# Sample attention with the probabilities as stationary operand in four column groups, and another order of the first loads and of x's transposes, squares and spills

## The chip, the cores and the metric

The kernel runs on one core of a Trainium2 chip. The core has five engines with queues of their own: PE (TensorE, the matrix unit; PEld is its weight load), DVE (VectorE), ACT (ScalarE), POOL (GpSimd) and SP (SyncE, which here only issues DMAs). Time is device time in microseconds (us) of one execution; smaller is better.

## The reference

One inference step of one hybrid decoder layer for a prompt of 512 tokens and for 8 sample sequences of 4 tokens (32 tokens). Everything is float32.

```python
h = rmsnorm(x)                                   # D = 1024
x_r, q, k, v, g_lru, g_attn = split(h @ w_in)    # 1024, 1024, 256, 256, 1024, 1024 columns
A = rg_lru(causal_conv4(x_r))                    # gated recurrence
B = window_attention(q, k, v)                    # 8 query heads, 2 kv heads, window 128, sinks,
                                                 # relative-position bias from rel_bias (32 buckets)
m = (sigmoid(g_lru) * (A @ w_lru_o) + sigmoid(g_attn) * (B @ w_attn_o)) @ w_out
x = x + rmsnorm(m)
u = causal_conv3(rmsnorm(x) @ w_up)              # 2 x 4096 columns
x = x + rmsnorm((gelu(u_gate) * u_val) @ w_down)
```

For a sample sequence the attention runs over 128 cached keys and values and its own 4 new ones, `o = softmax([q·k_cache, q·k_new] + bias) · [v_cache, v_new]`. The outputs are both groups' rows and their new states.

## The kernel before, in words

**Operands.** Activations lie transposed: features on the 128 partitions, the 544 tokens (512 + 32) in the free dimension, cut into a half of 256 (a = 0) and one of 288 (a = 1). To keep float32 precision, each operand is split into a high and a low part (`hH`, `hL`, `wh_in`, `wl_in`), and each product is made of three: high·high, low·high, high·low. ACT makes the high part, DVE subtracts it and so makes the low one.

**Steps.** The work on PE is a row of steps. `step(key, X, a, done)` is one column block of 128 of a weight matrix times one half of the tokens: 24 matmuls into one PSUM bank of the pool PM (3 banks; tiles `pmin`, `pmao` and so on). After a step comes `tick()`: it splits the next weight pieces (`wsplit_hi` on ACT, L277; `wsplit_lo` on DVE, L282), advances the side work (generators that `start_at(t, ...)` enters at tick t; a `yield` waits for the next tick), evicts the step's result, and at its end runs what was put in the list `last`. Side work takes its banks from the pool PX (5 banks). The written order is the order of each of PE, ACT, DVE and POOL; SP's order is made by a scheduler from the order and the dependencies of its DMAs.

**The start.** The first steps all use the half a = 0, which needs tiles 0 and 1 of x only (`trans_a`, in `first_step`). Their weight pieces are w16, w18, w8, w9, w10, w11 in this order (the numbers are column blocks; tiles `raw_in_...` of 512 KB). Tiles 2, 3 (prompt) and 4 (the 32 sample rows) are loaded in two half tiles of 512 columns each (`xload(i, z)`, z the half) and make the other half of the tokens: `trans_b` transposes them on PE, three transposes into one bank `ps_tb` for each of 8 feature blocks k, `hsplit` makes `hH` and `hL` of each, and `keep_b` copies the bank to an SBUF tile `xk`, which a POOL DMA spills to DRAM (`xtd`), where x is read again for the residual. `row_scales` makes the squares of x's rows and the roots of their means.

**The bias table.** One small product on PE (`ps_ohp`, from `ohp` and `relx`, in `attn_tables`, behind the third step) gives the biases by distance; DVE copies it (`rvec`), a POOL DMA writes it to DRAM (`rscr`), a second one repeats it there 128 times for each head (`rrep`), and a third loads it as `btab` for the attention (`load_btab`), whose first use of it is a DVE operation into `s`.

**The sample attention.** `sample_attn(g)` runs for two groups g of four sequences each, in side work. The scores of the group (`pss`) are a matmul with the 32 columns of one sequence's q as weights, for each of four column groups of PE's array. The probabilities are transposed (`pst`) and copied to `spt`. Then the output, transposed, is made in one bank `pso`: the new values for all sequences at once, and for each sequence b and kv head the cached values as 128x128 weights (`cache_win_v`), with the 16 probability columns of that pair as the moving operand. ACT and DVE then split the bank head by head into `aH` and `aL`, the operands of the attention output product (`pmao`).

Of the kernel before, what the change touches and what calls it, by code (L numbers as in the profile page):

```python
# [117 lines left out]
def hawk_step(ctx, tc, I, O):  # L118
# [21 lines left out]
    def T(name, dt=F32):  # L140
        return tp.tile([P, FLAT + 4], dt, tag="t", name=name)
# [7 lines left out]
    def PX(name):  # L149
        return psx.tile([P, 512], F32, tag="aux", name=name)  # L150
# [4 lines left out]
    def f32(ap):  # L155
        return ap.bitcast(F32)

    def mm(out, l, r, start, stop):
        pe.matmul(out, l, r, start=start, stop=stop)  # L159

    def sub(out, a, b):
        dve.tensor_tensor(out=out, in0=a, in1=b, op=ALU.subtract)  # L162
# [216 lines left out]
    relx = cp.tile([NBK + 1, NH], F32, name="relx")  # L379
    ohp = T("ohp")[:NBK + 1, 0:3 * WIN]  # L380

    pool.memset(relx, 1.0)
    nc.sync.dma_start(out=relx[0:NBK, :], in_=I["rel_bias"])
    nc.sync.dma_start(out=ohp, in_=I["c_ohp"])

    def table_loads():
        pool.memset(lt, 0.0)
# [27 lines left out]
    ss = cp.tile([P, 4, 5], F32, name="ss")  # L415
    dve.memset(ss, 1.0)
    rsc = cp.tile([P, 4], F32, name="rsc")
    rep = cp.tile([P, NT], F32, name="rep")
    xtd = drp.tile([KD, P, NT], F32, name="xtd")

    jk, jv = T("jk"), T("jv")

    def xsquares(i):
        n = TOK[i][1]
        act.activation(jk[:n, 0:512], xt[i, 0][:n, 0:512], AF.Square, accum_out=ss[:n, 0, i:i + 1])
        xb = xt[i, 1][:n, 0:512]
        dve.scalar_tensor_tensor(out=jv[:n, 0:512], in0=xb, scalar=1.0, in1=xb, op0=ALU.mult, op1=ALU.mult,
                                 accum_out=ss[:n, 1, i:i + 1])
# [4 lines left out]
    def hsplit(k, a, ps):  # L433
        g = pv[:, G_PRE + k:G_PRE + k + 1]
        act.activation(h.get(k, a, 0), ps, AF.Copy, scale=g)
        stt(h.get(k, a, 1), ps, g, f32(h.get(k, a, 0)), ALU.mult, ALU.subtract)

    def xkeep(ks, lo, hi, src, copy):

        n = hi - lo  # L440
        t_ = S(f"xk{ks.start}_{lo}")[:, 0:n * (2 if lo == 0 else 1)]
        copy(t_, src)
        pool.dma_start(out=xtd[ks, :, lo:hi].rearrange("k p n -> p k n"), in_=t_.rearrange("p (k n) -> p k n", n=n))

    pta = {}

# [14 lines left out]
    ptb = {}  # L461

    def keep_b(k):
        xkeep(slice(k, k + 1), 256, NT, ptb.pop(k)[:, :288], act.copy if k % 4 else dve.tensor_copy)

    def trans_b():
        for k in range(KD):
            ps = ptb[k] = (PM if k == 5 else PX)(f"ps_tb{k}")
            for i in (2, 3, 4):
                pe.transpose(ps[:, (i - 2) * P:(i - 1) * P], xtile(i, k), ident)  # L470
# [10 lines left out]
    def row_scales():  # L481
        last.extend(lambda i=i: xsquares(i) for i in range(2))
        yield 3
        last.extend(lambda i=i: xsquares(i) for i in range(2, 5))
# [4 lines left out]
        dg = T("dg_x")  # L489
        for i in range(5):  # L490
            w = TOK[i][1]
            dve.tensor_scalar(dg[:, i * P:i * P + w], ident[:, :w], ss[:, 1, i:i + 1], None, ALU.mult)
        yield 2
        px = [PX(f"ps_rep{a}") for a in range(2)]
        for a in range(2):
            mm(px[a][:, 0:HN], ones, dg[:, a * HN:(a + 1) * HN], True, True)
        for a in range(2):
            act.copy(rep[:, a * HN:(a + 1) * HN], px[a][:, 0:HN])

# [289 lines left out]
    def sample_attn(g):  # L789
# [54 lines left out]
        for hd in range(NH):  # L844
            oh, ol = (A.t[hd][z][:, SEQ + 16 * g:SEQ + 16 * g + 16].rearrange("p (b t) -> p b t", b=4)
                      for z in range(2))
            act.activation(oh, ov[:, :, hd, :], AF.Copy)
            sub(ol, ov[:, :, hd, :], f32(oh))
# [143 lines left out]
    def first_step():  # L992
        key = order[0]
        ps = PM("pm_first")
        def parts(z):
            split_a(z, range(1))
            lows = [wsplit_hi(w) for w in wclaim(z + 1)]
            split_a(z, range(1, 4))
            for v in lows:
                wsplit_lo(*v, pool)  # L1000

        k03, k47 = range(4), range(4, 8)
        trans_a(0)
        parts(0)
        mmhalf(ps, key, h, 0, k03, (0, 1))
# [837 lines left out]
```

## Time and profile before

| | before |
|---|---|
| time, median of 3 runs | 1014.81 us (1013.72, 1014.81, 1015.28) |
| time of the profiled execution | 1013.11 us |
| its span (first to last instruction) | 1011.0 us |
| mean granted clock of PE | 0.992 |
| PE busy | 990.1 us, 7817 instructions |
| DVE, ACT, POOL busy | 734.8, 597.4, 164.7 us |
| the pso records (32 of 128x16) | mean 0.263 us each, from 185.8 to 203.0 us |

The profiled execution is one run, 1.70 us below the median of the three. The times in the trace count from the start of its span. In the rows below, L159 is the helper that records every matmul, so a place is told by its tile: `pmin` is the input projection, `ps_ohp` the bias product, `ps_tb` the transposes of tiles 2 to 4, `pss` and `pso` the sample attention. A matmul of float32 shows as two records of the same tile, and a row with xN is a run of N records alike. "[1.09 <-DMA ohp...]" is idle time of the engine ahead of the row and what ended it. In rows of stretches of time the columns are: start and end, length, PE busy with the number of matmuls begun, granted clock (1.00 is full), busy share of the DMA engines, GB/s.

### The profile page before, as it was taken

What the parts mean: (1) busy time and instruction counts of PE and PEld (TensorE: products, weight loads), DVE (VectorE), ACT (ScalarE), POOL (GpSimd) and SP (SyncE); (2) the same over time, 40 slices, a digit from 0 to 9 for tenths busy, and PEclk for the clock granted to TensorE, in tenths of its full rate; (3) what the DMA queues carried; (4) which work ended last, traced back from release to release, by engine and by line L of the source; (5) the groups of instructions that cost most, each with busy time, mean ns of one, the idle gap of its engine ahead of it and who ended that gap; (6) DMA issues with size and microseconds to landing.
All of it is one profiled execution on the core that took longest, in us unless ns stands there. A gap on an engine that the chain in (4) does not pass through costs nothing.

```text
span 1011.0 us, 20259 instructions
## 1 busy us (share of the span) xinstructions
PE 990.1 (98%) x7817; PEld 980.5 (97%) x7817; DVE 734.8 (73%) x1535; ACT 597.4 (59%) x1448; POOL 164.7 (16%) x284
## 2 busy tenths in 40 slices
PE   8999999999999999999999999999999999999996
PEld 7999999999999999999999999999999999999996
DVE  4666666676856755578877788888888888878855
ACT  5645655666668535545866656565655555655644
POOL 4242000120404442200001111111110101011003
PEclk9999999999999999999999999999999999999998
DMA  9842223232322535225045858586767777675612
GB/s 264 255 166 85 81 64 105 84 105 84 85 84 85 172 104 145 71 74 182 22 123 130 186 131 192 124 191 130 185 142 172 152 162 162 152 180 136 190 57 89
DMA packets 209204, 134.00 MB, mean 133 GB/s; under 512 B 6664, under 2 KB 195481, under 8 KB 209076
## 3 DMA queue, kind: packets, MB, share of 16 engines
q1 hardware_dynamic: 198516, 110.08, 38.5%
q0 software_dynamic: 10240, 20.08, 11.7%
q10 hardware_dynamic: 352, 2.56, 0.6%
q8 instruction: 61, 1.00, 0.4%
q14 instruction: 35, 0.29, 0.1%
HBM read 111.30 MB, written 11.37 MB: 121 GB/s over the span
## 4 chain that ended last, share of the span: by engine, by line
PE 83%; DVE 6%; ACT 4%; DMA 3%; issue 2%; SPq 1%; POOL 0%; POOLq 0%; DVEq 0%; ACTq 0%
PE pmin L159 19%; PE pmdn L159 18%; PE pux L1452 14%; PE puy L1452 7%; PE pmao L159 5%; PE pmlo L159 4%; PE pmout L159 4%; PE puz L1452 4%; PE pq L1452 2%; PE psc L159 1%; DVE uc L171 1%; DMA raw_up_s<-in_w_up_dram 1%; PE pvp L159 1%; PE pg L159 1%; SPq L254 1%
## 5 line engine op out<-in xcount | busy, mean ns | idle before, releaser
L159 PE MATMUL pmin<-hH,wh_in 128*128 128x256 f32 (+1 forms) x568 | 165.6, 293 | 0.3 <-ACT gl L1031 0.3
L159 PE MATMUL pmin<-hH,wl_in 128*128 128x256 f32 (+1 forms) x568 | 163.2, 289 | 0.3 <-DVE wl_in L282 0.3
L159 PE MATMUL pmin<-hL,wh_in 128*128 128x256 f32 (+1 forms) x568 | 162.9, 289 | 0.0
L159 PE MATMUL pmdn<-fH,wh_dn 128*128 128x256 f32 (+1 forms) x512 | 148.0, 289 | 0.0
L159 PE MATMUL pmdn<-fH,wl_dn 128*128 128x256 f32 (+1 forms) x512 | 147.3, 288 | 0.4 <-DVE wl_dn L162 0.4
L159 PE MATMUL pmdn<-fL,wh_dn 128*128 128x256 f32 (+1 forms) x512 | 147.5, 288 | 0.0
L171 DVE SCALAR_TENSOR_TENSOR uc<-u,fv,uc 128x560 f32<-128x560 f32 x128 | 101.8, 796 | 11.0 <-ACT uc L1483 10.8
L159 PEld LDWEIGHTS pmin<-hH,wh_in 128*128 128x128 f32 x568 | 107.7, 190 | 2.1 <-issue 0.6
L159 PEld LDWEIGHTS pmin<-hL,wh_in 128*128 128x128 f32 x568 | 107.6, 190 | 0.0
L159 PEld LDWEIGHTS pmin<-hH,wl_in 128*128 128x128 f32 x568 | 107.0, 189 | 0.5 <-DVE wl_in L282 0.5
L159 PEld LDWEIGHTS pmdn<-fH,wl_dn 128*128 128x128 f32 x512 | 96.3, 188 | 0.7 <-DVE wl_dn L162 0.7
L159 PEld LDWEIGHTS pmdn<-fH,wh_dn 128*128 128x128 f32 x512 | 96.4, 188 | 0.1
L159 PEld LDWEIGHTS pmdn<-fL,wh_dn 128*128 128x128 f32 x512 | 96.3, 188 | 0.1
L1578 ACT COPY u<-pux 128x272 f32<-128x272 f32 x52 | 20.1, 386 | 84.7 <-PE pux L1452 84.7
L168 DVE TENSOR_TENSOR ft<-ft,pmdn 128x256 f32<-128x256 f32 (+1 forms) x112 | 48.5, 433 | 28.0 <-PE pmdn L159 28.0
L162 DVE TENSOR_TENSOR u<-puy,u 128x240 f32<-128x240 f32 (+2 forms) x78 | 24.6, 343 | 50.4 <-PE puy L1452 31.9
L277 ACT ACTIVATE wh_in<-raw_in 128x512 fp32r<-128x512 f32 x72 | 43.9, 627 | 10.7 <-DMA raw_in<-in_w_in_dram 6.3
L1483 ACT ACTIVATE uc<-u,fv 128x560 f32<-128x560 f32 x64 | 48.4, 755 | 1.8 <-DVE u L1459 1.8
L282 DVE TENSOR_TENSOR wl_in<-raw_in,wh_in 128x512 fp32r<-128x512 f32 x70 | 47.4, 694 | 0.0
L162 DVE TENSOR_TENSOR wl_dn<-raw_dn,wh_dn 128x512 fp32r<-128x512 f32 x64 | 43.7, 683 | 1.3 <-ACT wh_dn L1389 1.3
L1389 ACT ACTIVATE wh_dn<-raw_dn 128x512 fp32r<-128x512 f32 x64 | 39.7, 623 | 3.3 <-DMA raw_dn<-in_w_down_dram 3.3
L159 PE MATMUL pmlo<-lH,wh_lo 128*128 128x272 f32 x128 | 37.1, 290 | 1.3 <-ACT gl L1031 1.3
(747 smaller groups left out, 3323.4 us busy)
## 6 DMA issues: line engine op xcount, KB each, us to landing
raw_in<-in_w_in_dram SPq DMA_DIRECT2D x35, 512.0 KB
raw_dn<-in_w_down_dram SPq DMA_DIRECT2D x56, 256.0 KB
raw_up_s<-in_w_up_dram SPq DMA_DIRECT2D x26, 512.0 KB
raw_up_s<-raw_up_s POOLq DMA_DIRECT2D x26, 256.0 KB, 5.4
raw_ao<-in_w_attn_o_dram SPq DMA_DIRECT2D x8, 512.0 KB
raw_lo<-in_w_lru_o_dram SPq DMA_DIRECT2D x8, 512.0 KB
raw_out<-in_w_out_dram SPq DMA_DIRECT2D x8, 512.0 KB
x<-xtd SPq DMA_DIRECT2D x8, 272.0 KB
```

The source lines that it names most:

```text
L159: pe.matmul(out, l, r, start=start, stop=stop)
L162: dve.tensor_tensor(out=out, in0=a, in1=b, op=ALU.subtract)
L168: dve.tensor_tensor(out=out, in0=a, in1=b, op=ALU.add)
L171: dve.scalar_tensor_tensor(out=out, in0=a, scalar=s_, in1=b, op0=op0, op1=op1)
L254: nc.sync.dma_start(out=raw, in_=wsrc(key))
L277: act.activation(hl[0], raw, AF.Copy)
L282: (eng or dve).tensor_tensor(out=hl[1], in0=raw, in1=f32(hl[0]), op=ALU.subtract)
L1389: act.activation(hl[0], src, AF.Copy)
L1452: pe.matmul(ps[:, :HN], w, x, start=start and k == 0 and i == 0, stop=stop and k == 3 and i == 2, skip_group_check=True)
L1483: act.activation(yt[j][:, 0:FLATU], u[:, 0:FLATU], AF.Copy, scale=fv[:, j:j + 1])
L1578: act.copy(e[nm_], z)
```

## The change

**The first loads (SP).** `ohp` and `relx` are loaded ahead of and behind w8's piece, and tiles 2 to 4 of x by halves: the z = 0 halves ahead of w9's piece, the z = 1 halves ahead of w10's. In SP's queue, before; `raw_in_18` is w18's piece, and so on:

```order
L254 DMA raw_in_18_112<-in_w_in_dram 128x8x128
L254 DMA raw_in_8_114<-in_w_in_dram 128x8x128
L254 DMA raw_in_9_116<-in_w_in_dram 128x8x128
L254 DMA raw_in_10_118<-in_w_in_dram 128x8x128
L365 DMA x2_0_120<-in_x_prompt_dram 128x512
L365 DMA x2_1_122<-in_x_prompt_dram 128x512
L365 DMA x3_0_124<-in_x_prompt_dram 128x512
L365 DMA x3_1_126<-in_x_prompt_dram 128x512
L365 DMA x4_0_128<-in_x_sample_dram 32x512
L365 DMA x4_1_131<-in_x_sample_dram 32x512
L383 DMA relx_136<-in_rel_bias_dram 32x8
L384 DMA ohp_137<-in_c_ohp_dram 33x384
```

And there now:

```order
L254 DMA raw_in_18_115<-in_w_in_dram 128x8x128
L377 DMA ohp_102<-in_c_ohp_dram 33x384
L254 DMA raw_in_8_119<-in_w_in_dram 128x8x128
L378 DMA relx_101<-in_rel_bias_dram 32x8
L365 DMA x2_0_121<-in_x_prompt_dram 128x512
L365 DMA x3_0_123<-in_x_prompt_dram 128x512
L365 DMA x4_0_125<-in_x_sample_dram 32x512
L254 DMA raw_in_9_128<-in_w_in_dram 128x8x128
L365 DMA x2_1_130<-in_x_prompt_dram 128x512
L365 DMA x3_1_132<-in_x_prompt_dram 128x512
L365 DMA x4_1_134<-in_x_sample_dram 32x512
L254 DMA raw_in_10_137<-in_w_in_dram 128x8x128
```

The two small tables moved from behind all of these to the front, and w9's and w10's pieces moved behind halves of x. Behind the rows shown, w11's piece stands behind five small loads (`rows_b`) before, and behind four of them now.

**The transposes of tiles 2 to 4 (PE).** They come in groups of 9, 9 and 6 behind the third, fourth and fifth step, each group followed by its `xk` copies (four on ACT and four on DVE, before six and two); before, all 24 stood behind the fifth step. On PE, at the end of the third step (w8), before:

```order
L159 MATMUL pmin_8_0_356<-hH7_167,wl1_in_8_278 128x256
L159 MATMUL ps_ohp_389<-ohp_137,relx_136 8x384
L159 MATMUL pmin_9_0_399<-hH0_153,wh0_in_9_329 128x256
L159 MATMUL pmin_9_0_399<-hL0_154,wh0_in_9_329 128x256
L159 MATMUL pmin_9_0_399<-hH0_153,wl0_in_9_330 128x256
```

And there now:

```order
L159 MATMUL pmin_8_0_355<-hH7_167,wl1_in_8_281 128x256
L159 MATMUL ps_ohp_388<-ohp_102,relx_101 8x384
L481 MATMUL ps_tb0_394<-ident_88,x2_0_121 128x128
L481 MATMUL ps_tb0_394<-ident_88,x3_0_123 128x128
L481 MATMUL ps_tb0_394<-ident_88,x4_0_125 128x128
L481 MATMUL ps_tb1_400<-ident_88,x2_0_121 128x128
L481 MATMUL ps_tb1_400<-ident_88,x3_0_123 128x128
L481 MATMUL ps_tb1_400<-ident_88,x4_0_125 128x128
L481 MATMUL ps_tb2_406<-ident_88,x2_0_121 128x128
L481 MATMUL ps_tb2_406<-ident_88,x3_0_123 128x128
L481 MATMUL ps_tb2_406<-ident_88,x4_0_125 128x128
L159 MATMUL pmin_9_0_420<-hH0_153,wh0_in_9_328 128x256
```

Three banks of transposes now stand between the bias product and the fourth step (w9).

**Squares and spills.** The ACT squares of tiles 0 and 1 move into `first_step`, the others are spread over three ticks, and the roots go to the end of a tick. The spills of x are collected and issued by `xspill` one tick later: in POOL's queue seven of them now stand between the small table loads (`rel4`, `rows_a`) and `rscr`, and five behind `rrep`; before, four stood ahead of the table loads and eight behind `rrep`.

On DVE, ahead of the copy `rvec`, before (`wl..._10` are the low parts of w10's weights, L427 the squares):

```order
L282 TENSOR_TENSOR wl0_in_10_384<-raw_in_10_118,wh0_in_10_383 128x512
L282 TENSOR_TENSOR wl1_in_10_387<-raw_in_10_118,wh1_in_10_386 128x512
L427 SCALAR_TENSOR_TENSOR jv_175,ss_169<-x0_1_107 128x512
L427 SCALAR_TENSOR_TENSOR jv_175,ss_169<-x1_1_109 128x512
L584 COPY rvec_432<-ps_ohp_389 8x384
```

And there now:

```order
L282 TENSOR_TENSOR wl1_in_10_386<-raw_in_10_137,wh1_in_10_385 128x512
L171 SCALAR_TENSOR_TENSOR hL0_154<-ps_tb0_394,pv_141,hH0_153 128x288
L171 SCALAR_TENSOR_TENSOR hL1_156<-ps_tb1_400,pv_141,hH1_155 128x288
L171 SCALAR_TENSOR_TENSOR hL2_158<-ps_tb2_406,pv_141,hH2_157 128x288
L448 COPY xk0_256_412<-ps_tb0_394 128x288
L448 COPY xk2_256_416<-ps_tb2_406 128x288
L431 SCALAR_TENSOR_TENSOR jv_176,ss_169<-x0_1_110 128x512
L431 SCALAR_TENSOR_TENSOR jv_176,ss_169<-x1_1_112 128x512
L600 COPY rvec_460<-ps_ohp_388 8x384
```

Three low parts and two copies of the first group of transposes now stand between w10's weights and `rvec`.

**The sample attention (PE, DVE, ACT).** Stationary and moving operand change places: for each sequence and kv head the weights are the 32 probability columns of the sequence, written to rows 32b to 32b+31 of the bank, and the cached values are the moving operand of 128 columns. The output comes out untransposed, so DVE copies the bank (`so`), PE transposes it (`psa`), DVE copies that (`sa`), and the splits read `sa`, first the eight on ACT, then the eight on DVE. On PE, for the first group, before:

```order
L159 MATMUL pmin_1_1_2598<-hH7_167,wl1_in_1_2388 128x288
L159 MATMUL pso0_2630<-spt0_2584,vnt_197 128x128
L159 MATMUL pso0_2630<-spt0_2584,cache_win_v0_2134 128x16 x8
L159 MATMUL pmin_2_0_2656<-hH0_153,wh0_in_2_2445 128x256
L159 MATMUL pmin_2_0_2656<-hL0_154,wh0_in_2_2445 128x256
```

And there now, with the rows two steps further on behind the gap:

```order
L159 MATMUL pmin_1_1_2598<-hH7_167,wl1_in_1_2388 128x288
L159 MATMUL pso0_2630<-vnt_198,spt0_2584 128x128
L159 MATMUL pso0_2630<-cache_win_v0_2134,spt0_2584 32x128 x8
L159 MATMUL pmin_2_0_2656<-hH0_153,wh0_in_2_2445 128x256
...
L159 MATMUL pmin_2_1_2707<-hH7_167,wl1_in_2_2510 128x288
L861 MATMUL psa0_2739<-ident_88,so0_2692 128x128
L842 MATMUL pst1_2741<-ident_88,ss1_2640 128x128
```

The count of matmuls stays, their width goes from 16 to 128 columns, and one transpose for each group is added two steps later.

The diff, cut to its core:

```diff
+    relx = cp.tile([NBK + 1, NH], F32, name="relx")
+    ohp = T("ohp")[:NBK + 1, 0:3 * WIN]
+    pool.memset(relx, 1.0)
     xload(0, 0)
 ...
-    for i in range(1, 5):
-        wload(i)
-    for i in (2, 3, 4):
-        for z in range(2):
+    wload(1)
+    nc.sync.dma_start(out=ohp, in_=I["c_ohp"])
+    nc.sync.dma_start(out=relx[0:NBK, :], in_=I["rel_bias"])
+    wload(2)
+    for z in range(2):
+        for i in (2, 3, 4):
             xload(i, z)
+        wload(3 + z)
     wload(5)
 ...
-        pool.dma_start(out=xtd[ks, :, lo:hi]...)
+        kept_x.append((xtd[ks, :, lo:hi]..., t_...))
+
+    def xspill():
+        for o_, t_ in kept_x:
+            pool.dma_start(out=o_, in_=t_)
+        kept_x.clear()
 ...
-    def trans_b():
-        for k in range(KD):
-            ps = ptb[k] = (PM if k == 5 else PX)(f"ps_tb{k}")
+    def trans_b(ks):
+        for k in ks:
+            ps = ptb[k] = PX(f"ps_tb{k}")
             for i in (2, 3, 4):
                 pe.transpose(ps[:, (i - 2) * P:(i - 1) * P], xtile(i, k), ident)
             hsplit(k, 1, ps[:, :288])
-            if k >= 2:
-                keep_b(k - 2)
+        for k in ks:
+            keep_b(k)
 
     def side_b():
-        last.append(trans_b)
+        for ks in (range(0, 3), range(3, 6), range(6, 8)):
+            last.append(lambda ks=ks: trans_b(ks))
+            yield
         yield
-        keep_b(6)
-        keep_b(7)
+        xspill()
 ...
-        o = po[:, 0:P]
-        mm(o, vnt, pt[:64, 2 * P:3 * P], True, False)
-        for b in range(4):
-            for kv in range(NKV):
-                c0 = b * 32 + kv * 16
-                mm(o[:, c0:c0 + 16], vraw[:, b, kv * HD:(kv + 1) * HD],
-                   pt[:, kv * P + c0:kv * P + c0 + 16], False, b == 3 and kv == NKV - 1)
-        yield
-        ov = o.rearrange("p (b h t) -> p b h t", b=4, h=NH)
+        mm(po[:, 0:HD], pt[:64, 2 * P:3 * P], vnt, True, False)
+        for kv in range(NKV):
+            for b in range(4):
+                mm(po[32 * b:32 * b + 32, 0:HD], pt[:, kv * P + 32 * b:kv * P + 32 * b + 32],
+                   vraw[:, b, kv * HD:(kv + 1) * HD], False, kv == NKV - 1)
+        yield
+        so = T(f"so{g}")
+        dve.tensor_copy(so[:, 0:HD], po[:, 0:HD])
+        yield
+        px = PX(f"psa{g}")
+        pe.transpose(px[:, 0:P], so[:, 0:HD], ident)
+        yield
+        sa = T(f"sa{g}")[:, 0:P]
+        dve.tensor_copy(sa, px[:, 0:P])
+        ov = sa.rearrange("p (b h t) -> p b h t", b=4, h=NH)
 ...
-    start_at(FIRST - 1, side_b())
-    start_at(FIRST - 3, row_scales())
+    start_at(3, side_b())
+    start_at(3, row_scales())
+    start_at(4, once(xspill))
```

More of the change, by code (lines that the diff above doesn't have):

```diff
@@ L372, in hawk_step @@
     wraw_parts(0, (1,))
-    for i in range(1, 5):
-        wload(i)
-    for i in (2, 3, 4):
-        for z in range(2):
+    wload(1)
[4 more added lines that the diff above has]
+        for i in (2, 3, 4):
             xload(i, z)
+        wload(3 + z)
     wload(5)
[L379 to L384, printed above, removed]
     def table_loads():
@@ L417, in hawk_step @@
     rsc = cp.tile([P, 4], F32, name="rsc")
+    dg_x = T("dg_x")
     rep = cp.tile([P, NT], F32, name="rep")
@@ L421, in hawk_step, with xsquares @@
     jk, jv = T("jk"), T("jv")
-    def xsquares(i):
+    def xsquares(i, zs=(0, 1)):
         n = TOK[i][1]
[L425 to L428, printed above, removed]
+        for z in zs:
+            xb = xt[i, z][:n, 0:512]
+            if z == 0:
+                act.activation(jk[:n, 0:512], xb, AF.Square, accum_out=ss[:n, 0, i:i + 1])
+            else:
+                dve.scalar_tensor_tensor(out=jv[:n, 0:512], in0=xb, scalar=1.0, in1=xb, op0=ALU.mult,
+                                         op1=ALU.mult, accum_out=ss[:n, 1, i:i + 1])
     def xtile(i, k):
@@ L436, in hsplit @@
         stt(h.get(k, a, 1), ps, g, f32(h.get(k, a, 0)), ALU.mult, ALU.subtract)
+    kept_x = []
     def xkeep(ks, lo, hi, src, copy):
@@ L442, in xkeep @@
         copy(t_, src)
-        pool.dma_start(out=xtd[ks, :, lo:hi].rearrange("k p n -> p k n"), in_=t_.rearrange("p (k n) -> p k n", n=n))
+        kept_x.append((xtd[ks, :, lo:hi].rearrange("k p n -> p k n"), t_.rearrange("p (k n) -> p k n", n=n)))
+    def xspill():
+        for o_, t_ in kept_x:
+            pool.dma_start(out=o_, in_=t_)
+        kept_x.clear()
     pta = {}
@@ L463, in keep_b @@
     def keep_b(k):
-        xkeep(slice(k, k + 1), 256, NT, ptb.pop(k)[:, :288], act.copy if k % 4 else dve.tensor_copy)
-    def trans_b():
-        for k in range(KD):
-            ps = ptb[k] = (PM if k == 5 else PX)(f"ps_tb{k}")
+        xkeep(slice(k, k + 1), 256, NT, ptb.pop(k)[:, :288], act.copy if k % 2 else dve.tensor_copy)
+    def trans_b(ks):
+        for k in ks:
+            ps = ptb[k] = PX(f"ps_tb{k}")
             for i in (2, 3, 4):
@@ L471, in trans_b, with roots @@
             hsplit(k, 1, ps[:, :288])
-            if k >= 2:
-                keep_b(k - 2)
+        for k in ks:
+            keep_b(k)
     def side_b():
-        last.append(trans_b)
+        for ks in (range(0, 3), range(3, 6), range(6, 8)):
+            last.append(lambda ks=ks: trans_b(ks))
+            yield
         yield
-        keep_b(6)
-        keep_b(7)
[L481 to L484, printed above, removed]
-        yield
+        xspill()
+    def roots():
         add(ss[:, 0, :], ss[:, 0, :], ss[:, 1, :])
@@ L488, in row_scales @@
         dve.tensor_scalar(rsc, ss[:, 1, 0:4], SCALE, None, ALU.mult)
-        dg = T("dg_x")
         for i in range(5):
             w = TOK[i][1]
-            dve.tensor_scalar(dg[:, i * P:i * P + w], ident[:, :w], ss[:, 1, i:i + 1], None, ALU.mult)
+            dve.tensor_scalar(dg_x[:, i * P:i * P + w], ident[:, :w], ss[:, 1, i:i + 1], None, ALU.mult)
+    def row_scales():
+        last.extend(lambda i=i: xsquares(i, (1,)) for i in range(2))
+        yield 2
+        last.append(lambda: xsquares(2))
+        yield
+        last.extend(lambda i=i: xsquares(i) for i in (3, 4))
+        yield
+        last.append(roots)
         yield 2
@@ L834, in sample_attn @@
         po = PX(f"pso{g}")
-        o = po[:, 0:P]
-        mm(o, vnt, pt[:64, 2 * P:3 * P], True, False)
-        for b in range(4):
-            for kv in range(NKV):
-                c0 = b * 32 + kv * 16
-                mm(o[:, c0:c0 + 16], vraw[:, b, kv * HD:(kv + 1) * HD],
-                   pt[:, kv * P + c0:kv * P + c0 + 16], False, b == 3 and kv == NKV - 1)
-        yield
-        ov = o.rearrange("p (b h t) -> p b h t", b=4, h=NH)
[L844 to L848, printed above, removed]
+        mm(po[:, 0:HD], pt[:64, 2 * P:3 * P], vnt, True, False)
[3 more added lines that the diff above has]
+                   vraw[:, b, kv * HD:(kv + 1) * HD], False, kv == NKV - 1)
+        yield
+        so = T(f"so{g}")
[3 more added lines that the diff above has]
+        pe.transpose(px[:, 0:P], so[:, 0:HD], ident)
+        yield
+        sa = T(f"sa{g}")[:, 0:P]
+        dve.tensor_copy(sa, px[:, 0:P])
+        ov = sa.rearrange("p (b h t) -> p b h t", b=4, h=NH)
+        for z in range(2):
+            for hd in range(NH):
+                oh, ol = (A.t[hd][j][:, SEQ + 16 * g:SEQ + 16 * g + 16].rearrange("p (b t) -> p b t", b=4)
+                          for j in range(2))
+                if z == 0:
+                    act.activation(oh, ov[:, :, hd, :], AF.Copy)
+                else:
+                    sub(ol, ov[:, :, hd, :], f32(oh))
     stage = cp.tile([P, KD, 36], F32, name="stage")
@@ L1004, in first_step @@
         parts(0)
+        for i in range(2):
+            xsquares(i, (0,))
         mmhalf(ps, key, h, 0, k03, (0, 1))
```

2 lines of the change are left out of this document (1 added, 1 removed).

## The prediction

> **What bounds the kernel now.** I read the busy times first, then the chain of waits, then what PE (TensorE) waits for.
>
> ```profile
> PE 990.1 (98%) x7817; PEld 980.5 (97%) x7817; DVE 734.8 (73%) x1535; ACT 597.4 (59%) x1448; POOL 164.7 (16%) x284
> PE 83%; DVE 6%; ACT 4%; DMA 3%; issue 2%; SPq 1%; POOL 0%; POOLq 0%; DVEq 0%; ACTq 0%
> ```
>
> PE is busy for 990.1 of a span of 1011.0 us and carries 83% of the chain. So a microsecond comes back only in two ways: PE stops waiting somewhere, or it needs less time for the same work. The list of PE's waits (tile, line, what ended it; sum, count, longest, us) has two that the change touches:
>
> ```profile
> PE ps_tb L470 <- ACT xk L442: 1.2, 1, 1.2
> PE ps_ohp L159 <- DMA ohp<-in_c_ohp_dram: 1.1, 1, 1.1
> ```
>
> PE's own timeline (start, length of the run, line, operation) gives what surrounds them:
>
> ```profile
> 19.70 0.28 PE L159 MATMUL pmin<-hH,wl_in 128*128 128x256 f32 x1
> 21.07 0.80 PE L159 MATMUL ps_ohp<-ohp,relx 33*8 33x384 f32 x2 [1.09 <-DMA ohp<-in_c_ohp_dram]
> 21.80 0.39 PE L159 MATMUL pmin<-hH,wh_in 128*128 128x256 f32 x1
> 22.03 0.28 PE L159 MATMUL pmin<-hL,wh_in 128*128 128x256 f32 x1
> ...
> 27.60 2.13 PE L470 MATMUL ps_tb<-ident,x 128*128 128x128 f32 x18
> 30.92 0.91 PE L470 MATMUL ps_tb<-ident,x 128*128 128x128 f32 x6 [1.19 <-ACT xk L442]
> 31.58 0.36 PE L159 MATMUL pmin<-hH,wh_in 128*128 128x256 f32 x1
> ```
>
> Ends are modelled, so I count from start to start. The third place shows as busy time; it is the p·V product of the sample attention (pso), beside the score product (pss), whose weights are already 32 columns wide:
>
> ```profile
> 164.28 0.64 PE L159 MATMUL pss<-kcT,qs 128*32 128x256 f32 x8
> 164.84 0.40 PE L159 MATMUL pmin<-hH,wh_in 128*128 128x288 f32 x1
> 185.84 1.96 PE L159 MATMUL pso<-spt,cache_win_v 128*128 128x16 f32 x16
> 187.65 0.37 PE L159 MATMUL pmin<-hH,wh_in 128*128 128x256 f32 x1
> 201.32 1.96 PE L159 MATMUL pso<-spt,cache_win_v 128*128 128x16 f32 x16
> 203.13 0.37 PE L159 MATMUL pmin<-hH,wh_in 128*128 128x256 f32 x1
> ```
>
> The fourth is no wait either. In stretches of 3.40 us (PE busy, count, granted clock, DMA share, GB/s) PE looks fully busy, yet once here it does 18 matmuls where 28 fit, at a clock of 0.50:
>
> ```profile
> 9.20:12.60 3.40, 3.40 (x17) 0.50 1.22 290
> 26.30:29.70 3.40, 3.40 (x31) 1.00 0.76 211
> 29.70:33.10 3.40, 2.21 (x20) 1.00 1.13 303
> 186.70:190.10 3.40, 3.40 (x31) 1.00 0.63 189
> 190.10:193.50 3.40, 3.40 (x29) 1.00 0.26 77
> 200.40:203.80 3.40, 3.40 (x28) 1.00 0.00 0
> 203.80:207.20 3.40, 3.40 (x18) 0.50 0.80 228
> ```
>
> **The change part by part.**
>
> *The bias product.* The last matmul ahead of it starts at 19.70, so PE could go on at 19.82 (one pitch of 0.12, as matmuls of 256 columns have); it starts at 21.07. Its table and weights (ohp, relx) are now loaded ahead of w8's and behind it instead of behind everything, so they are there long before 19.82. Gain 1.25 us.
>
> *The transposes of tiles 2 to 4.* The block lasts from 27.60 to 31.58, 3.98 us for 24. The last six alone take 31.58 − 30.92 = 0.66, 0.11 each, so 24 need 2.64; the rest, 1.34, is the wait for a free bank. Split into three groups they cost two more change-overs to the step's matmuls, which the first matmul behind the bias product prices: 22.03 − 21.80 = 0.23 where the pitch is 0.12, so 0.11 each. Gain 1.1.
>
> Where that wait comes from stands in the chain, in order of time (start, length, what):
>
> ```profile
> 13.51 6.57 DMA x<-in_x_prompt_dram
> ...
> 21.11 5.04 DMA raw_in<-in_w_in_dram
> 26.17 1.15 ACT wh_in L277 x2
> ...
> 28.05 1.20 DVE wl_in L282 x2
> ...
> 30.47 0.41 ACT xk L442
> ```
>
> SP waited for an x load to land (20.08) before it could issue on, so the sixth weight piece went out at 21.11 and landed at 26.15; its split held ACT and DVE, and the copy that frees the bank came last. In the new SP order the load that stands as many places ahead of that piece, x2_1, ends after 2.42 MB instead of 3.07 (weights 512 KB, half tiles 256 KB each, from w18's piece on): 0.65 MB at the 290 GB/s of the first row above are 2.2 us, so the piece goes out near 19 and lands near 24, ahead of its step.
>
> Now the same clock forwards: bias product 19.82 to 20.55; nine transposes to 21.6; a step takes (27.60 − 21.80)/2 = 2.90, to 24.5; nine transposes to 25.6; a step to 28.5; six transposes to 29.2. The sixth step started at 31.58, so 2.35 come back, the sum of the two gains.
>
> *What is late next.* The fifth weight piece (w10) now has the bytes ahead of it that ohp had, so it lands near 21.0 (the bias product's start in the trace):
>
> ```profile
> 28.13 1.67 ACT L435 ACTIVATE hH<-ps_tb,pv 128x288 fp32r<-128x288 f32 x4 [0.26 <-PE ps_tb L470]
> 29.50 1.35 DVE L171 SCALAR_TENSOR_TENSOR hL<-ps_tb,pv,hH 128x288 fp32r<-128x288 f32 x3
> ```
>
> ACT: 21.0 + 1.15 for the split, about 0.3 for evicting the step's result, three high parts at 1.67/4 = 0.42, one copy 0.41: 24.1. DVE: the low halves (1.20, the second behind ACT's) to 23.0, three low parts (1.35) to 24.4, one copy, taken as ACT's: 24.8. The fifth and sixth transposed tiles need those banks at 24.8 to 25.2. So the wait is 0 to 0.2, and 1 us if the piece lands 1 us later; I take 0.1. The squares and copies that moved run on ACT and DVE, whose cover is PE's steps of 2.90 each; the moved spills are POOL's DMAs, which nobody on PE waits for. They also put POOL's queue in another order, ahead of the bias table (last rival).
>
> *The p·V product.* A block takes 187.65 − 185.84 = 1.81 us and 203.13 − 201.32 = 1.81, for 16 records of 16 columns, 0.113 each: the same 0.11 that 128 columns cost above, so 16 columns save nothing. The new form streams 16 × 128 = 2048 columns with 32-column weights. The nearest row, pss, does 8 × 256 = 2048 columns so in 164.84 − 164.28 = 0.56. Bounds: 0.56 if four column groups run side by side as there, 16 × 0.113 = 1.81 if they don't. I take 0.56, since its four groups are laid out alike. Added on PE: a transpose, 0.11, and a change-over, 0.11. Gain 1.81 − 0.56 − 0.22 = 1.03 a block, 2.05 for both. The two DVE copies and ticks that follow lie beside steps; the result is used some 20 us later, in the attention output product.
>
> *The clock.* Of the two blocks one lies within a single stretch, 200.40 to 203.80, and the next stretch is at half clock; the other is cut by the border at 186.70, and no slow stretch follows. So I read it that 1.8 us of 16-column matmuls in one stretch count as too little work. A half-clock stretch does 1.7 us of work in 3.4. With blocks of 0.56 us at 128 columns I expect it to go: gain 1.7; bounds 0 and 1.7.
>
> [...]
>
> **The sum.** 1.25 + 1.1 − 0.1 + 2.05 + 1.7 = 6.0 us. The profiled execution took 1013.11, so 1007.1. The median shown, 1014.81, is 1.70 above it, just one half-clock stretch; which stretches fall on which work varies, and if the second block's cost runs in both blocks, the median gives 1014.81 − 7.7 = 1007.1 as well, otherwise 1008.8. I take 1008.0, with 1005.9 to 1009.5 as this case's own range.
>
> **The rivals.**
> [...]
> (b) The early gain is eaten by the next late thing: w10 1 us late, or the bias table (below) by up to 2.6. For: slack in the sum above is 0.2. 1009.0 to 1010.6.
> (c) The column groups don't overlap, say because the stationary side's change in width stops them: 2 × (1.03 + 0.22) = 2.5 less, and the low activity stays: 1010.5 to 1012.2. Against: pss.
> (d) The early loads land no sooner, since the DMA engines are full (share above 1 in the rows) and the change only exchanges who waits: 2.35 less, 1010.4. Against: ohp and relx are tiny and only their place in the queue matters.
> (e) Slower. The bias table is made on a chain over DRAM:
>
> ```profile
> 21.91 0.55 DVE L584 COPY rvec<-ps_ohp 8x384 f32<-8x384 f32 x1 [1.05 <-PE ps_ohp L159]
> 23.82 0.50 POOL L585 DMA_DIRECT2D rscr<-rvec  x1 [0.25 <-DMA rel<-in_rel_bias_dram]
> 28.22 1.13 POOL L588 DMA_DIRECT2D rrep<-rscr  x1 [3.91 <-DMA rscr<-rvec]
> rrep<-rscr POOLq DMA_DIRECT2D x1, 1536.0 KB, 14.9
> 44.23 0.73 POOL L616 DMA_DIRECT2D btab<-rrep  x1
> DMA to landing us min/median/max: 3.6/4.9/6.2
> 51.98 0.47 DVE L171 SCALAR_TENSOR_TENSOR s<-psc,rsc,btab 128x256 f32<-128x256 f32 x1
> 55.01 0.18 DVE L165 TENSOR_TENSOR qs<-pmin,rep 128x32 f32<-128x32 f32 x1
> 57.97 0.28 PE L159 MATMUL pmin<-hH,wh_in 128*128 128x256 f32 x1
> ```
>
> The copy of the bias rows (rvec) now stands on DVE behind w10's late split, three low parts and two x copies, done at 25.2 by the sums above, and then two squares; it ends near 27.0 instead of 22.46. From there to the table's landing took 44.23 + 6.2 − 22.46 = 28.0, so it could come at 55.0. DVE holds PE's bank for 3.2 us from its use of the table at 51.98 to 55.19, and PE wants the bank at 57.97, now 55.6: a start after 52.4 stalls PE, so 55.0 costs 2.6, which is in (b). It decides the sign only if the table comes after about 61, 6 us beyond the worst from the rows; against it, the transfers near 44 are shorter than the 14.9 one that shared the DMA with the weights. Then 1017 or more.
>
> **How the numbers follow.** All works: 0.50; (a) 0.18; (b) 0.15; (c) 0.07; (d) 0.05; (e) 0.05. About 0.2% (2.0 us) is what a measurement of this kernel can tell from no change. All but (e), and (c) where it ends at its upper end, are below 1012.8; allowing 0.06 for the runs' own 1.7 either way: faster 0.88, same 0.07, slower 0.05. The range, 1005.9 to 1011.2, takes in (a), (b), (d) and half of (c).
>
> **What would show it.** Right: no wait for ohp or xk ahead of 31 us, and the sixth step's first matmul near 29.2; pso's 16 records in 0.6 us; a clock of 1.00 throughout 180 to 210. Wrong: pso at 0.11 a record; a half-clock stretch behind the pso blocks or behind the transposes; PE idle at 24.5 to 25.5 with xk as its releaser; DVE waiting for btab at 52 to 55.

## The result and the profile after

| | before | after |
|---|---|---|
| median of 6 runs each | 1014.26 us (1012.69 to 1015.96) | 1006.21 us (1005.80 to 1009.07) |
| ratio, 95% interval | | 0.9938 (0.9922 to 0.9953) |
| median of the second comparison, 11 and 6 runs | 1012.63 us | 1007.81 us |
| its ratio, 95% interval | | 0.9947 (0.9926 to 0.9968) |
| profiled execution, span | 1013.11, 1011.0 us | 1006.24, 1004.5 us |
| mean granted clock there | 0.992 | 0.997 |

The change takes 0.5 to 0.6% off: 8.05 us by the first medians, 4.82 by the second and 6.87 between the two profiled executions. 1006.21 is 1.8 below the predicted 1008.0 and 0.3 inside the lower end of the range. The busy times, from the page of the profile after:

```profile
PE 984.5 (98%) x7819; PEld 974.0 (97%) x7819; DVE 736.0 (73%) x1541; ACT 595.9 (59%) x1446; POOL 165.4 (16%) x284
```

PE is busy for 5.6 us less, with two matmuls more. Neither ps_ohp nor ps_tb is in the list of PE's waits any more. PE's timeline at the start, and at the two blocks of the sample attention (start, length of the run, line, operation):

```profile
18.91 0.28 PE L159 MATMUL pmin<-hH,wl_in 128*128 128x256 f32 x1
19.12 0.81 PE L159 MATMUL ps_ohp<-ohp,relx 33*8 33x384 f32 x2
19.86 1.20 PE L481 MATMUL ps_tb<-ident,x 128*128 128x128 f32 x9
20.82 0.36 PE L159 MATMUL pmin<-hH,wh_in 128*128 128x256 f32 x1
...
28.13 0.36 PE L159 MATMUL pmin<-hH,wh_in 128*128 128x256 f32 x1
...
182.62 0.64 PE L159 MATMUL pso<-cache_win_v,spt 128*32 128x128 f32 x16
183.19 0.39 PE L159 MATMUL pmin<-hH,wh_in 128*128 128x256 f32 x1
...
196.98 0.64 PE L159 MATMUL pso<-cache_win_v,spt 128*32 128x128 f32 x16
197.55 0.39 PE L159 MATMUL pmin<-hH,wh_in 128*128 128x256 f32 x1
```

The sixth step starts at 28.13, before at 31.58: 3.45 earlier. A block of 16 records takes 183.19 − 182.62 = 0.57 us, before 1.81. Two of the stretches looked at before, and the two in which PE now waits for the row statistics that are taken between the steps of the output product (pst_f; length, PE busy, count, granted clock, DMA share, GB/s):

```profile
9.20:12.60 3.40, 3.12 (x20) 1.00 1.16 304
203.80:207.20 3.40, 3.40 (x31) 1.00 0.49 141
418.86:422.27 3.41, 2.83 (x23) 1.00 0.00 0
422.27:425.69 3.42, 2.32 (x19) 1.00 0.35 95
```

The clock is 1.00 in all of them; in this execution it is 1.00 from 5.9 to 999.1 us and 0.50 only behind that, when PE's last matmul (started at 996.17) is done. Before, it was 0.50 in the first two and in a third, not shown so far:

```profile
429.10:432.50 3.40, 2.23 (x18) 1.00 0.32 90
432.50:435.90 3.40, 3.40 (x17) 0.50 0.24 69
```

There PE waits in the first stretch for pst_f, 1.67 us as in the changed kernel (1.68), and has the half clock in the next. In the profile after, a border of the 3.41-us grid cuts the same wait at 422.27, and no half clock follows.

How far PE is ahead of before at the same instruction, from the two timelines, shows where the time came from and where some of it went:

| place on PE | before, us | after, us | ahead by |
|---|---|---|---|
| bias product starts | 21.07 | 19.12 | 1.95 |
| sixth step starts | 31.58 | 28.13 | 3.45 |
| first pso block starts / ends | 185.42 / 187.65 | 182.20 / 183.19 | 3.22 / 4.46 |
| second pso block starts / ends | 200.91 / 203.13 | 196.56 / 197.55 | 4.35 / 5.58 |
| first gate matmul (pg) | 228.78 | 221.91 | 6.87 |
| end of the output product | 443.46 | 435.00 | 8.46 |
| last matmul of the kernel | 1002.70 | 996.17 | 6.53 |

1.9 us of the 8.46 are lost again, 1.85 of them near 920 us, a place that the last part of the experiments looks at.

### The profile page after: what moved, and what is told of

Its sections match the earlier page's. It is cut to its first block, busy times and chain, and to the rows that moved or that the text cites. A ratio compares the mean times of both kernels' runs of the same rounds, so it can differ in the third digit from the quotient of the medians.

```text
span 1004.5 us, 20266 instructions
## 1 busy us (share of the span) xinstructions
PE 984.5 (98%) x7819; PEld 974.0 (97%) x7819; DVE 736.0 (73%) x1541; ACT 595.9 (59%) x1446; POOL 165.4 (16%) x284
## 4 chain that ended last, share of the span: by engine, by line
PE 84%; DVE 6%; ACT 4%; issue 2%; DMA 2%; POOL 1%; POOLq 0%; DVEq 0%; ACTq 0%
PE pmdn L159 18%; PE pmin L159 18%; PE pux L1480 14%; PE puy L1480 7%; PE pmao L159 5%; PE pmlo L159 5%; PE pmout L159 4%; PE puz L1480 4%; PE pq L1480 3%; DMA raw_up_s<-in_w_up_dram 1%; PE psc L159 1%; DVE uc L171 1%; PE pvp L159 1%; PE pg L159 1%; DVE hs L958 1%
## 5 line engine op out<-in xcount | busy, mean ns | idle before, releaser
L1406 POOL DMA_DIRECT2D raw_up_s<-raw_up_s x26 | 22.3, 857 | 98.4 <-issue 4.7
```

Of the source, the lines that this page charges most:

```text
L1406: pool.dma_start(out=w["p4"], in_=w["p2"], accum_op=ALU.add)
```

## The experiments

Apart from a kernel's time, two readings are used. One is the lead over before at a place of PE's timeline, as in the table above. The other is the clock's loss of an execution, (1 − mean granted clock) × span, which is known for every run: 5.6 us on average over 35 runs of before, and 3.0 and 3.4 over twice 6 runs of the changed kernel. In each of the 14 profiles 1.7 to 2.8 us of this loss lie behind PE's last matmul, where they cost PE nothing; a half-clock stretch ahead of that counts 1.7, half of its 3.41. Times are compared with runs of before on the same chip; the chip is not the same for all experiments, so across experiments only the ratios can be compared.

**The early part alone.** The kernel before with all edits of the change except those in `sample_attn`.

> The change's order of loads, transposes, squares and spills, with the old sample attention. Theory (two separate sources of time, and the clock on top): PE reaches the sixth step 2.7 us sooner, as in the trace of the changed kernel (9.01 us from bias product to sixth step instead of 11.76), and nothing of it is given back: 0.997 of the time before. A half-clock stretch stays behind a pso block in most runs. Rival (the early gain is given back later, at the bias table): under 1 us of it reaches the end, and PE waits between 45 and 60 us.

1011.06 us against 1013.22, ratio 0.9982 (0.9967 to 0.9997): less than expected, 2.2 us by the medians. The lead is 3.32 us at the sixth step: 0.67 from a full clock near 9 us, and the 2.7 of the theory (whose 11.76 counts from 19.82, where the product could have started, not from 21.07). It is 3.06 at the second pso block, 4.55 at the end of the output product (before lost 1.4 to the half clock near 204; here the blocks left the clock full this time), and 3.56 at the end. The bias table costs nothing here. The loss lies elsewhere: of 4.37 us at the 915th microsecond of before, 3.51 are left at the 956th, which neither theory had. The clock's loss is 6.4 us over the 12 runs, not below the 5.6 of before.

This profile also tests the prediction's reading of the clock. Its first pso block, of the old form, lies whole in one stretch (182.33 to 184.56), and the next stretch is at full clock:

```profile
181.22:184.63 3.41, 3.41 (x28) 1.00 0.50 146
184.63:188.05 3.42, 3.42 (x30) 1.00 0.55 161
```

**The sample attention alone.** The kernel before with the change's `sample_attn`.

> The change's sample attention alone, with the old start. Theory: each pso block takes 1.0 instead of 1.8 us with its first product counted, so 1.1 us come back at each of two places, and the half-clock stretch behind a block goes (1.7, or 3.4 where there were two): 2.2 + 1.7 = 3.9 us, 0.996. Rival (the clock has nothing to do with the blocks): a half-clock stretch stays somewhere near 200 us and the gain is 2.2, 0.998. Bias product and transposes wait as before, 1.1 and 1.2 us.

1010.76, ratio 0.9978 (0.9962 to 0.9994). The ratio is the rival's 0.998, not the theory's 0.996. At the place itself the theory holds: each block brings 1.23 us (PE is 0.20 us behind before at the start of the first block and 1.04 ahead at its end, then 0.87 and 2.10 ahead at the second), about 0.1 of it goes to its transpose two steps later, as expected, and the clock stays full around 204. Bias product and transposes wait 0.6 and 1.7 us. Again 1.15 us are lost near 920, so 2.2 remain of 3.4. The clock's loss is 5.1 us over the 12 runs, hardly below 5.6: this profile has a half-clock stretch from 8.13 to 11.55 and one behind pst_f, as before has. With the clock's loss taken out, the mean falls by 1.4 us; for the early part alone it falls by 2.0.

**The order of the loads alone.** The edit, shortened:

```diff
 # before, with the change's order of the first DMAs on SP; trans_b, row_scales, xkeep as before
+    wload(1); ohp; relx; wload(2); x2_0, x3_0, x4_0; wload(3); x2_1, x3_1, x4_1; wload(4); wload(5)
```

> The change's order of the first loads alone; the 24 transposes stay in one block. Theory: the wait of the bias product goes (1.25 us); the block still waits for a free bank, since its eight high and low parts go through ACT and DVE at 0.4 us each and only six banks are there: 0.5 to 1.0 us of the old 1.2 stay. Gain 1.3 to 1.9. Rival (the wait in the block came from w11's late landing alone): the wait goes too, and the gain is 2.4 or more.

1011.13, ratio 0.9973 (0.9956 to 0.9989). The block of transposes in PE's timeline:

```profile
28.29 0.91 PE L470 MATMUL ps_tb<-ident,x 128*128 128x128 f32 x6 [0.44 <-ACT xk L442]
28.95 0.36 PE L159 MATMUL pmin<-hH,wh_in 128*128 128x256 f32 x1
```

The bias product no longer waits. Of the 1.19 us in the block 0.44 stay, a little under the 0.5 to 1.0 of the theory, so both the late piece and the block's own traffic through six banks made that wait. The sixth step leads by 2.63 us, three quarters of the changed kernel's 3.45; 0.70 of it is there ahead of the bias product already, from the full clock near 9 us.

**The groups alone.** All of the early part, but the loads in the old order.

> The grouped transposes, squares and spills alone, with the old order of loads. Theory: the bias product waits as before (1.1 us); the wait in the block goes, since a group finds its banks free: gain 1.0 to 1.4. Rival (the groups need the new loads): ACT and DVE stand behind the split of a weight piece that has not landed, with a group's copies queued behind it, PE waits for a bank and the gain is below 0.5.

1015.11, ratio 1.0010 (0.9994 to 1.0025): no gain, and neither theory had the reason. PE at the bias product and the first group, and the stretches there:

```profile
21.96 0.80 PE L159 MATMUL ps_ohp<-ohp,relx 33*8 33x384 f32 x2 [1.71 <-DMA ohp<-in_c_ohp_dram]
22.69 2.02 PE L481 MATMUL ps_tb<-ident,x 128*128 128x128 f32 x9
```
```profile
19.50:22.91 3.41, 1.70 (x11) 1.00 0.60 162
22.91:26.33 3.42, 3.42 (x18) 0.50 0.96 303
```

No transpose waits for a bank, so the groups do what they should. But ohp landed later, PE was idle for 1.71 us of the stretch that ends at 22.91, and the next one got half the clock: nine transposes took 2.0 us instead of 1.2. 0.9 later, 1.5 saved, some 1.7 lost: the sixth step is 0.97 behind before. The clock's loss over the 12 runs is 6.6 us, against 5.6. Here the groups did not pay, with the product ahead of them waiting.

**The clock behind narrow matmuls and behind transposes: a ladder of each.** Both are the changed kernel with extra work on PE whose result is not used; the edit, shortened:

```diff
             mmhalf(ps, key, X, a)
+            if 26 <= nstep < 101 and nstep % 3 == 0:      # m cycles through 6, 8, 10, 12, 14
+                for _ in range(m):                        # second kernel: 2*m transposes of 128x128
+                    mm(spare[:, 0:16], w[:, 0:128], w[:, 128:144], True, True)
```

> The changed kernel with extra work on PE whose result is not used: behind every third step from the 27th to the 99th, a block of 6, 8, 10, 12 or 14 matmuls of 16 columns into a spare bank, 1.4, 1.8, 2.3, 2.7 and 3.2 us by the 0.113 us of a pso record. Theory (the clock follows the work in a stretch of the 3.41 us grid, counted in columns streamed): in the traces so far the stretches ahead of a half-clock one had 3270 columns or fewer and those with 3536 or more never had one behind them; a full stretch has about 7300. A block of 1.4 us leaves some 4600 and triggers nothing; one of 1.8 leaves 3750 and seldom does, without a product beside it; 2.7 and 3.2 us trigger wherever they lie in one stretch, about every second block or fewer; each costs 1.7 us. Rival (only idle time counts): PE is never idle in these blocks, and no half-clock stretch appears between 100 and 430 us.

> The same as the kernel with the blocks of 16 columns, but each block is 12, 16, 20, 24 or 28 PE transposes of 128x128, which take as long (0.11 us each). Theory (columns count): even 28 of them in one stretch stream 3584 columns, so few or no half-clock stretches between 100 and 430 us. Rival (transposes do not count as busy): the same number of half-clock stretches as with the 16-column blocks, behind the longest.

1074.31 and 1060.26 us, for the same count of records. One block of 28 records in each, PE's row and the grid stretch with it and the one behind; first the narrow matmuls:

```profile
386.54 3.47 PE L159 MATMUL lad<-hH 128*128 128x16 f32 x28
```
```profile
385.90:389.31 3.41, 3.41 (x32) 1.00 0.95 327
389.31:392.72 3.41, 3.41 (x17) 0.50 0.33 97
```

and the transposes:

```profile
374.87 3.22 PE L353 MATMUL lad<-ident,hH 128*128 128x128 f32 x28
```
```profile
374.52:377.93 3.41, 3.41 (x33) 1.00 0.94 308
377.93:381.34 3.41, 3.41 (x30) 1.00 0.32 92
```

Of the 25 narrow blocks the 8 with 2.30 us or more inside one stretch (from the first record's start to the last's) were all followed by half clock, the 17 with 2.04 us or less never. Of the 25 blocks of transposes none was, though five had 2.4 to 2.9 us in one stretch. PE shows no idle time in the blocks of either. So here the half clock came without any idle time of PE, behind records of 16 columns (28 of them are 448), and not behind as many transposes of 128 (3584). Before has both: 3.40 us busy of 3.40 in the stretch ahead of its half clock at 203.80, and 2.1 us of transposes in the stretch from 26.30, with 1.00 in the next. That it is the columns that decide, and nothing else in which the two ladders differ, is my reading of these runs.

**The order inside the p·V product.** The changed kernel with its two loops exchanged.

```diff
-        for kv in range(NKV):
-            for b in range(4):
+        for b in range(4):
+            for kv in range(NKV):
```

> The changed kernel with the two loops of the p-V product exchanged: both kv heads of a sequence, and so of a column group, stand one behind the other. Theory (the column groups run side by side only while neighbours in the queue use different groups; four records, one for each, started within 20 ns in the changed kernel, and then four more every 0.11 us): the block's 16 records take 0.9 to 1.8 us instead of 0.57. Rival (PE starts what is free whatever the order): 0.57 again.

1006.52 in its one run. The first block:

```profile
183.27 0.67 PE L159 MATMUL pso<-cache_win_v,spt 128*32 128x128 f32 x16
183.87 0.39 PE L159 MATMUL pmin<-hH,wh_in 128*128 128x256 f32 x1
```

0.60 us instead of 0.57, where 16 records at 0.11 would take 1.8: the rival is right, the records overlap here in either order.

**The changed kernel again.**

> The changed kernel again, on the same chip and with more runs. Theory (early start, sample attention and clock add up): with the granted clock taken out, 1.7 to 2.0 us from the early part and 1.4 to 2.2 from the sample attention, 3.1 to 4.2 in all; the clock's own loss falls from 5.6 us to about 3, so 0.994 again. Rival (the clock's loss is chance and the same in both): 0.9965.

1007.81, ratio 0.9947. With the clock's loss taken out of each run, the mean falls from 1007.4 to 1004.5, 2.9 us, a little below the 3.1 to 4.2 expected, and the clock's loss from 5.7 to 3.4, as the theory had it. Its profile shows a wait that the first one did not have, in DVE's timeline and in PE's list of waits between 40 and 62 us:

```profile
52.11 0.48 DVE L171 SCALAR_TENSOR_TENSOR s<-psc,rsc,btab 128x256 f32<-128x256 f32 x1 [3.62 <-DMA btab<-rrep]
```
```profile
PE pmin L159 <- DVE qs L165: 0.8, 1, 0.8
```

That is the bias table of the prediction's rivals (b) and (e), and DVE waiting for btab at 52 to 55 is one of the signs that the prediction gave for being wrong. The next two runs move it.

**The bias rows one tick earlier, and one tick later.**

```diff
     def attn_tables():
         mm(ps[:NH, 0:3 * WIN], relx, ohp, True, True)
-        yield                       # earlier: no yield; later: yield 2
```

> The changed kernel with the copy of the bias rows (rvec) and the first two DMAs of the bias table one tick earlier, ahead of w10's split on DVE and of the spills on POOL. Theory (the table's chain over DRAM is the next thing that can be late): rvec ends near 20.5 instead of 26.2, the table is there before 48.6, DVE does not wait for it (2.2, 3.1 and 3.6 us in the profiles so far), and PE never waits for qs near 54 (0.8 us in one profile, 0.2 in another, 0 in the rest): 0 to 0.8 us faster than the changed kernel with the clock taken out. Rival (the 1.5 MB that the second DMA writes then meets the first weights): a weight piece lands later and PE waits 0.5 us or more before 45 us.

> The changed kernel with that copy one tick later. Theory: rvec ends 3 to 4 us later, the table is first used at 54 to 56 instead of 50.8 to 52.1, and PE waits 2.5 to 4.5 us for qs between 54 and 60, since it stalls when that use begins after 51.3 (52.11 cost 0.8, 51.81 cost 0.2). Rival (the chain absorbs it, since the DMAs then run in a quieter time): the use moves by less than 2 us.

DVE's copy of the bias rows and the first use of the table, in the changed kernel's first profile:

```profile
25.64 0.54 DVE L600 COPY rvec<-ps_ohp 8x384 f32<-8x384 f32 x1
50.84 0.48 DVE L171 SCALAR_TENSOR_TENSOR s<-psc,rsc,btab 128x256 f32<-128x256 f32 x1 [2.20 <-PE pv L694]
```

with the copy earlier:

```profile
20.09 0.55 DVE L599 COPY rvec<-ps_ohp 8x384 f32<-8x384 f32 x1 [1.61 <-PE ps_ohp L159]
50.35 0.47 DVE L171 SCALAR_TENSOR_TENSOR s<-psc,rsc,btab 128x256 f32<-128x256 f32 x1
```

and later, with PE's wait:

```profile
28.89 0.54 DVE L600 COPY rvec<-ps_ohp 8x384 f32<-8x384 f32 x1
53.25 0.48 DVE L171 SCALAR_TENSOR_TENSOR s<-psc,rsc,btab 128x256 f32<-128x256 f32 x1 [4.22 <-DMA btab<-rrep]
```
```profile
PE pmin L159 <- DVE qs L165: 1.4, 1, 1.4
```

5.6 us earlier, DVE no longer waits for the table and PE waits nowhere near 54 us; no weight piece came late for PE either, so that rival fell. 3.2 us later (1009.21 us in its one run), the use comes 2.4 us after the first profile's, between the rival's less than 2 and the theory's 54 to 56, and PE waits 1.4 us, less than the 2.5 to 4.5 expected; the DMA that spreads the rows took 12.4 instead of 13.4 us. Use at 50.84, 52.11 and 53.25 cost PE 0, 0.8 and 1.4 us. The chain is as the prediction described it, with little slack. In time the earlier copy shows nothing: 1007.72, ratio 0.9958 (0.9944 to 0.9972), against 0.9947 for the changed kernel on another chip. That is no proof of no gain; 0.8 us in some runs is below what these intervals tell.

**Filling the wait for pst_f, in the output product.**

```diff
+        if nm == "f0":
+            for _ in range(12):
+                pe.transpose(ps[:, 0:P], ident, ident)
         for z in range(nch):
             mm(ps[:, z:z + 1], acc[:, z * P:(z + 1) * P], ones[:, 0:1], ...)
```

> The changed kernel with 12 PE transposes whose result is not used in the idle 1.7 us ahead of the row statistics behind the output product (pst_f, near 430 us). Theory (a stretch with too few columns brings the half clock): they take 1.3 us of the idle time, so nothing is later, and lift the stretch from 1640 to 3270 columns to 3200 to 4800: the half-clock stretch behind pst_f, there in most profiles so far, goes in most runs, and with it 1.0 to 1.7 us. Rival (transposes do not count, or the wait itself does it): the half-clock stretch stays, no gain.

The stretch with that wait and the one behind it, in the second profile of the changed kernel:

```profile
421.95:425.36 3.41, 1.73 (x15) 1.00 0.03 11
425.36:428.77 3.41, 3.41 (x17) 0.50 0.51 145
```

and with the wait filled:

```profile
421.29:424.70 3.41, 3.06 (x27) 1.00 0.17 44
424.70:428.11 3.41, 3.41 (x28) 1.00 0.37 112
```

As the theory had it, the clock is 1.00 in both; its loss is 1.7 us over six runs, where the second six of the changed kernel had 3.4 (in the profile all of it lies behind PE's last matmul), and PE leads by 8.97 us at the end of the output product. Yet the time is 1007.38, ratio 0.9948 (0.9930 to 0.9966), no better than the changed kernel's 0.9947. The lead at the end is 6.11: 2.7 us are gone near 920.

**Both together.**

> The early bias rows and the filled wait together, in the changed kernel. Theory: both gains add up, 1 to 2.5 us faster than the changed kernel, 1004.5 to 1006 median. Rival: neither shows beyond the runs' spread, 1006 to 1008.

1008.21, ratio 0.9957 (0.9940 to 0.9975): neither gain shows, as the rival had it, though its 1006 to 1008 is just missed. The clock's loss is 2.2 us, the lead 8.16 behind the output product and 4.23 at the end.

**Where the lead goes.** The loss sits in the last two pieces of the up projection, whose transfer ends the chain there. The transfers in the chain, in order of time (start, length, what), before:

```profile
907.16 5.09 DMA raw_up_s<-in_w_up_dram
922.48 5.23 DMA raw_up_s<-in_w_up_dram
```

after:

```profile
898.86 6.66 DMA raw_up_s<-in_w_up_dram
915.76 5.54 DMA raw_up_s<-in_w_up_dram
```

in the kernel with the loops exchanged:

```profile
901.11 5.35 DMA raw_up_s<-in_w_up_dram
916.70 4.86 DMA raw_up_s<-in_w_up_dram
```

and with both edits:

```profile
899.61 6.87 DMA raw_up_s<-in_w_up_dram
916.71 6.73 DMA raw_up_s<-in_w_up_dram
```

Against before, the two transfers took 1.9 us more after, 0.1 less with exchanged loops and 3.3 more with both edits; the lead lost between the 915th and the 956th microsecond of before was 1.9, −0.1 and 3.3. The three other profiles whose chain holds both transfers agree: 0.5 us less and 0.5 won with the loads alone, 0.6 and 0.6 with the groups alone, 2.8 and 2.7 with the wait filled. After, DVE waits for each of them:

```profile
905.62 0.69 DVE L168 TENSOR_TENSOR p<-raw_up_s,raw_up__12310 128x512 f32<-128x512 f32 x1 [2.06 <-DMA raw_up_s<-in_w_up_dram]
921.32 0.69 DVE L168 TENSOR_TENSOR p<-raw_up_s,raw_up__12505 128x512 f32<-128x512 f32 x1 [2.41 <-DMA raw_up_s<-in_w_up_dram]
```

Before, the first of these waits was 0.46 us and the second 2.06. PE then waits for what ACT and DVE make behind these pieces, 1.2 us in all between 900 and 945 us before (0.8 and 0.4 in the same two places of its list) and 2.7 after:

```profile
PE pux L1480 <- ACT u L1606: 1.7, 2, 0.9
PE pmdn L159 <- DVE wl_dn L162: 1.0, 2, 0.5
```

So that is a second bound behind PE, and its size varies with the execution: the changed kernel lost 1.9 and 1.3 us there in its two profiles, its twin with exchanged loops nothing. That the lead is lost where these transfers are long is shown; why they are longer in some executions, and whether an earlier PE makes them so, is open.

## Why the prediction was right, and where its terms were off

| term | predicted | measured in the profiles |
|---|---|---|
| wait of the bias product | 1.25 | 1.16 (lead from 0.79 to 1.95) |
| transposes of tiles 2 to 4 | 1.1 | 1.50 (lead from 1.95 to 3.45) |
| new wait for w10 | −0.1 | none on PE |
| two pso blocks, with the transposes added | 2.05 | 2.28 (1.24 and 1.23, less 0.11 and 0.08) |
| half clock behind the second block | 1.7 | 1.49 (lead from 5.58 to 7.07) |
| not foreseen: half clock at 9.2 | 0 | 0.79, ahead of the bias product |
| not foreseen: half clock at 432.5 | 0 | 1.59 |
| not foreseen: last up-projection transfers | 0 | −1.93 |
| small losses between these places | 0 | −0.35 |
| sum, in the profiled execution | 6.0 | 6.53 on PE, 6.5 of span, 6.87 of time |

The waits. Both went as argued, and the new order of loads is what makes it so: with loads alone the bias product no longer waits and the sixth step leads by 2.63 us, with groups alone it is 0.97 behind. The bias product starts 0.21 us behind the matmul ahead of it, not the pitch of 0.12 that the sum took. The transposes were undersized by 0.4 us; the change-overs that I charged to the groups don't show as a loss, since from bias product to sixth step PE takes 9.01 us where my sum had 9.4.

The sample attention. The choice of the pss row as the price was right to 0.01 us a block, 0.57 against 0.56. The first product of the block, with the new keys' values, takes 0.42 us in both kernels, so leaving it out of the sum changed nothing. The transpose with its change-over was charged with 0.22 us a block and cost 0.11 and 0.08.

The clock. The prediction read one block of 1.8 us in one stretch as too little work. That it can bring the half clock is borne out, that it must is not. In the four profiles with the old sample attention four blocks have 17 or 18 of their 18 records in one stretch: two of these stretches, with 2656 and 2624 columns (before and loads alone), are followed by half clock, and two, with 2784 and 3200 (the early part and the groups alone), are not; nor is any of the four blocks that a border cuts. In the eight profiles with the new blocks and no work added near them, no half clock follows one. So 1.7 was the price in one execution and not in every run. A step that failed is that I looked at this one stretch only. The one from 9.20 stands among my rows, but the sum has nothing for it, and the one from 432.5 I did not show at all. The first is there in all three profiles with the old order of loads (it begins at 8.1 to 9.3) and in none of the eleven with the new one; by what the order of loads does this, no run shows. The second was luck: nine of the twelve profiles in which PE's wait for pst_f is not filled have it, the changed kernel's second one too. Over all runs the clock's loss fell by 2.3 to 2.6 us with the whole change, yet with neither part alone (6.4 and 5.1 against 5.6); why it takes both is open.

Rival (a), that the slow stretch stays or appears elsewhere, fell. Rival (b) was half right: the bias table costs PE 0.8 us in one of two profiles of the changed kernel, and in the other its chain took 24.7 us from rvec's end to first use where I had bounded the time to the table's landing by 28.0. Rivals (c) and (d) fell: the new block takes 0.57 us, and with the loads alone the bias product no longer waits. Rival (e) did not decide; the copy another 3.2 us later costs only 1.4 us on PE.

The sum failed in one more step: it let every microsecond on PE reach the end. 1.9 us don't, near 920, and the unforeseen gain in the clock (2.4) about covers that. So the total came out nearer than its terms, and that part is luck; that the waits and the two blocks would give what they gave is not.

## What to carry to other kernels

A wait on the first transfers was cheapest cured in the queue, by putting the few kilobytes that PE needs first ahead of the megabytes it needs later; spreading the work that follows paid only on top of that. Small matmuls on a narrow moving operand cost a full slot each here (0.113 us for 16 columns, 0.11 for 128), so put the short side in the stationary operand, in column groups that run side by side (16 records in 0.57 us here). Ahead of counting a gain on the bound engine, look for the next bound behind it, here two weight transfers 700 us later, and let its slack cap the sum.

## What the runs showed of the hardware

- PE's clock fell to 0.50 for the 3.41 us behind a stretch of 3.41 us that held 2.30 us or more of the added 16-column matmuls, once for two such lengths (119.65 to 126.47), though PE was never idle in those blocks; 2.04 us or less of them did not do it, nor did up to 2.9 us of transposes. The three half-clock stretches of before, at 9.20, 203.80 and 432.50, lie 57 and 67 times 3.41 us apart, and so I speak of a grid.
- Counting columns streamed in each stretch at full clock over the 14 profiles (a full one has about 7300; the first 4 and the last 12 us left out): 17 of 18 stretches below 2500 were followed by half clock, 6 of 20 between 2500 and 3300, none of 44 between 3300 and 4000. Between 2500 and 3300 the count alone did not decide in these profiles.
- The mean granted clock differs from run to run of one kernel: 35 runs of before on one chip lay between 1009.86 and 1018.63 us, with mean clocks of 0.997 and 0.990 at these ends, and 7.1 of the 8.8 us between them are the clock's loss.
